# All eleven column groups of the second SwiGLUs by seven products, the first prepared during the mixer's output projection

## The chip, the cores and the metric

The kernel runs on one core of one Trainium2 chip. The metric is the device time of one execution in microseconds, as the median of several runs. A profiled execution comes with a trace of every instruction: TensorE (PE in the rows: matmuls, and PEld, their weight loads), VectorE (DVE), ScalarE (ACT), GpSimd (POOL) and the DMA queue that SyncE (SP) issues.

## The reference

Two layers work on 512 tokens of width 1024, in float32. What matters here is what stands around the second SwiGLU of each layer:

```python
h = h + merged @ w_o[i]                                                   # end of the mixer
h = h + 0.5 * swiglu(rmsnorm(h, ffn2_norm[i]), ffn2_w_gu[i], ffn2_w_down[i])
gate = jax.nn.sigmoid(rmsnorm(h, ple_norm[i]) @ w_ple_gate[i])

def swiglu(x, w_gu, w_down):
    g, u = jnp.split(x @ w_gu, 2, axis=-1)                                # 1024 -> 2 x 2816
    return (jax.nn.silu(g) * u) @ w_down                                  # 2816 -> 1024
```

## The kernel before

The activations lie transposed: `h[0]` to `h[7]` are 128 features by 512 tokens each, and a weight tile of 128x128 is the stationary operand. Each float32 product is made of three matmuls on rounded halves: a value is split into a rounded high part and the rest, and hi*hi, hi*lo and lo*hi are added up in PSUM (`mm3`, L266). The high part is a copy on ScalarE (L71, L260, L263), the low part a subtraction on VectorE (L72, L261, L264). Weights come as tiles of 128x1024 (512 KB, `Stream.raw`) into ten buffers (tag `st`, which the weight sums `s` use too), and the split ones lie in four pairs of buffers (`wh`, `wl`, `N_WH = 4`). So a new weight split on ScalarE waits until TensorE has read the split of four tiles before.

A SwiGLU has 22 blocks of 128 gate columns and as many up columns. Two neighbouring blocks, gate and up, make a **quad**: `Sevens` computes it by Strassen's way with seven products instead of eight, on halves of the inner dimension, of the tokens (256 and 256) and of the columns. `Quad` loads four quarters of the weights and forms four sums of them on VectorE (`part`: L149, L152, L154, L157). `Halved.row` makes the sums of the tokens: row j takes `h[j]` and `h[j+4]`, `own` the part that needs `h[j]` alone and `other` the rest; eight such operations on ScalarE and twelve on VectorE end in the split operands. `Sevens.step(n, j)` makes product j of quad n. Products 1, 2, 6, 3 and 4 are `joint`: 8 matmuls of 512 columns (L527: the weights' high part against the high and the low part of 256 tokens side by side) and 8 of 256 columns (L533: the low part). Products 5 and 7 are `product`, 24 matmuls of 256 columns each (L547).

The products of a quad share sums. `step` gathers product 1 in a PSUM pair `b`, copies it on ScalarE into the pair `a` (`seed`, L552) and adds product 2 there; product 6 goes on in `b`, which is then copied into the pair `d` for products 5 and 3; 7 and 4 end in `b`. `a` and `d` are the same two PSUM banks (pool `ap`, one buffer), so the seed of the one waits until the other has been read out (`out`, L556 on ScalarE and L557 on VectorE). After that `finish` scales by the norm's factor `r`, applies silu, multiplies (L603, L604, L608) and splits the result for the down projection. `down(m, f0, f1)` preloads a PSUM bank with 2*`h[m]` (L640), adds blocks f0 to f1 and writes `h[m]` back halved (L644); `fill` makes one such piece between two products of a quad. `next_quad` orders the steady part: quad n's product 4 stands behind quad n+1's product 1, and fills stand behind 4, 6 and 3.

Except in the very first SwiGLU, two of the 22 blocks (0 and 1) are not done by a quad but whole: `projs` and `proj` make 4 x 8 x 3 = 96 matmuls of 512 columns. Block 0 stands at the start of the SwiGLU, block 1 in two halves between the products of the first quad: whole gate and up of block 0, norm, 1 of quad 1, gate of block 1, 2 and 6, up of block 1, 5, 7, 3. The rest are ten quads.

Before that the mixer's output projection makes eight products of 24 matmuls (L1058 to L1060), `m0wop` in layer 0: each adds its result to `h[m]` on VectorE (L1060). As each `h[m]` is done, `normed` splits it (L263, L264), squares it (L333, L336), adds up the squares (L337), and, from `h[4]` on, makes two of the four token rows (`early=2`). `rms` turns the sum of squares into the factor `r` by two matmuls and a chain of ScalarE and VectorE operations (L350 to L354), with a load of an activation table ahead of it.

The order of each engine's instructions is set when the program is built, by a scheduler that may move an instruction ahead of others that it expects to wait; on the chip each engine takes its instructions in that order.

Of the kernel before, what the change touches and what calls it, by code (L numbers as in the profile page):

```python
# [129 lines left out]
class Quad:  # L130


    def __init__(self, W, quarters):
        self.W = W
        for q in ("a11", "a21", "a22", "a12"):
            setattr(self, q, W.raw(quarters[q]))

    def part(self, j):

        W = self.W  # L140
        tt = W.nc.vector.tensor_tensor
        if j == 1:
            return W.split(self.a11)
        if j == 2:
            return W.split(self.a12)
        if j == 4:
            return W.split(self.a22)
        if j == 3:
            tt(self.a12, self.a12, self.s, ALU.subtract)  # L149
            return W.split(self.a12)  # L150
        if j == 6:
            tt(self.a11, self.a11, self.a21, ALU.subtract)  # L152
# [6 lines left out]
        return W.split(self.a11)  # L159


# [21 lines left out]
def trunk_kernel(ctx, tc, dims, x, p, positions, gains, rope_c, final_row, weights, out):  # L183
# [19 lines left out]
    class Banks:  # L203


        def __init__(self):
            self.scope, self.n = None, 0
# [148 lines left out]

    def normed(nm, l, name, after=None, paired=True):

        xs, sq = [], Squares(name)
        for k in range(KD):  # L360
            xs.append(split(h[k], f"{name}x{k}", gain(nm, l, k), paired))
            sq.add(h[k])
            if after:
                after(k, xs)
        return xs, sq.parts()
# [130 lines left out]
    class Sevens:  # L496
# [62 lines left out]

        def step(self, n, j):  # L560
            d, H = self.quad(n), self.H
            if j == 1:
                d["b"] = PB(f"{self.name}{n}b")
                self.joint(d["b"], d, j)
                self.seed(n, "a")
            elif j == 2:
# [20 lines left out]

    def ffn(l, nm, name, first=False, beside=iter(()), early=2):

# [4 lines left out]
        ys = Halved(nm, l, name)  # L594
        n_whole = 4 if first else 2
        n0 = n_whole // 2
# [25 lines left out]

        xs, acc = normed(nm, l, name, early_rows)

# [26 lines left out]
        def fill():  # L651
            if downs:
                m, f0 = downs.pop(0)
                down(m, f0, f0 + 4)
# [12 lines left out]

# [9 lines left out]
        if first:  # L677
# [22 lines left out]
            activate(3)  # L700
            downs.extend((m, 0) for m in range(KD))
            fill()
# [5 lines left out]
            for _ in range(2):  # L708
                fill()
        else:  # L710
            pss[0] = whole(0)
# [18 lines left out]
        f0 = f_last  # L730
        left = [m for m in range(KD) if (m, f0) in downs]
        assert len(left) == len(downs)
# [25 lines left out]
    def mixer(l):  # L758
# [298 lines left out]
        banks.paired()  # L1057
        for m in range(KD):  # L1058
            ps = proj(W.col("w_o", l, m * P, D), merged, f"{name}wop{m}")
            nc.vector.tensor_tensor(h[m], ps, h[m], ALU.add)  # L1060
# [249 lines left out]
```

## Time and profile before

| what | us |
|---|---|
| median of 3 runs (2252.12 to 2252.79) | 2252.23 |
| profiled execution, its own time | 2252.33 |
| its span, first to last instruction | 2250.3 |
| busy: PE / DVE / ACT | 2240.8 / 1743.5 / 1456.1 |
| matmuls | 12144 |
| output projection of layer 0's mixer | 685.6 to 729.1 |
| start of the second SwiGLU of layer 0, to the end of its first quad's product 3 | 729.1 to 768.5 |

The page says 100% for PE, but a busy PE is not PE at its peak: a matmul of 512 columns is shown with 389 ns, and the next one starts some 227 ns later. So the starts of neighbouring matmuls are what to read. A row of the timeline has its start in us from the start of the span, its length, engine, line and operation; behind it in brackets the idle time before it and what ended it. Neighbours on ACT and DVE overlap by about 0.1 us, so that their spacing is the length less that.

### The profile page before, as it was taken

What the parts mean: (1) busy time and instruction counts of PE and PEld (TensorE: products, weight loads), DVE (VectorE), ACT (ScalarE), POOL (GpSimd) and SP (SyncE); (2) the same over time, 40 slices, a digit from 0 to 9 for tenths busy, and PEclk for the clock granted to TensorE, in tenths of its full rate; (3) what the DMA queues carried; (4) which work ended last, traced back from release to release, by engine and by line L of the source; (5) the groups of instructions that cost most, each with busy time, mean ns of one, the idle gap of its engine ahead of it and who ended that gap; (6) DMA issues with size and microseconds to landing.
All of it is one profiled execution on the core that took longest, in us unless ns stands there. A gap on an engine that the chain in (4) does not pass through costs nothing.

```text
span 2250.3 us, 31142 instructions
## 1 busy us (share of the span) xinstructions
PE 2240.8 (100%) x12144; PEld 1947.7 (87%) x12144; DVE 1743.5 (77%) x2453; ACT 1456.1 (65%) x2246; POOL 37.4 (2%) x42
## 2 busy tenths in 40 slices
PE   9999999999999999999999999999999999999998
PEld 8888888888888888888888888888888888888887
DVE  8987768788866887776798777687889678777756
ACT  7666666576744666667676666764767357666664
POOL 0000000000200000000000000000001000000000
PEclk9999999999999999999999999999999999999999
DMA  5333332323132232334223233323222223333321
GB/s 215 99 113 104 103 122 75 112 76 104 47 104 84 94 103 97 107 107 141 75 94 104 96 106 108 113 88 102 92 76 75 94 75 103 104 104 103 108 99 38
DMA packets 63362, 223.04 MB, mean 99 GB/s; under 512 B 7280, under 2 KB 7280, under 8 KB 63216
## 3 DMA queue, kind: packets, MB, share of 16 engines
q1 hardware_dynamic: 62640, 220.28, 29.2%
q8 instruction: 95, 1.56, 0.3%
q10 hardware_dynamic: 576, 0.79, 0.1%
q14 instruction: 51, 0.42, 0.1%
HBM read 218.94 MB, written 2.10 MB: 98 GB/s over the span
## 4 chain that ended last, share of the span: by engine, by line
PE 97%; DVE 2%; ACT 1%; issue 0%; DVEq 0%
PE a0pd L268 2%; PE a1pd L268 2%; PE b0pd L268 2%; PE b1pd L268 2%; PE a0pd L269 2%; PE a0pd L270 2%; PE b1pd L269 2%; PE b0pd L269 2%; PE a1pd L269 2%; PE b1pd L270 2%; PE b0pd L270 2%; PE a1pd L270 2%; PE m0mop L268 1%; PE m1mop L269 1%; PE m0mop L269 1%; PE m1mop L270 1%
## 5 line engine op out<-in xcount | busy, mean ns | idle before, releaser
L72 DVE TENSOR_TENSOR wl<-st,wh 128x1024 fp32r<-128x1024 f32 (+1 forms) x508 | 614.7, 1212 | 227.5 <-ACT wh L71 224.1
L71 ACT CAST wh<-st 128x1024 fp32r<-128x1024 f32 (+1 forms) x507 | 527.9, 1044 | 306.6 <-PE m1Bp L269 13.9
L71 ACT CAST wh<-s 128x1024 fp32r<-128x1024 f32 x49 | 51.6, 1052 | 28.8 <-PE m1Cp L269 4.2
L72 DVE TENSOR_TENSOR wl<-s,wh 128x1024 fp32r<-128x1024 f32 x49 | 59.6, 1216 | 0.3 <-ACT wh L71 0.3
L152 DVE TENSOR_TENSOR st<-st,st 128x1024 f32<-128x1024 f32 x49 | 59.7, 1219 | 0.2
L154 DVE TENSOR_TENSOR s<-st,st 128x1024 f32<-128x1024 f32 x49 | 59.6, 1217 | 0.1
L149 DVE TENSOR_TENSOR st<-st,s 128x1024 f32<-128x1024 f32 x49 | 59.6, 1216 | 0.0
L157 DVE TENSOR_TENSOR st<-st,st 128x1024 f32<-128x1024 f32 x49 | 59.6, 1216 | 0.0
L644 ACT ACTIVATE h<-a0pd 128x512 f32<-128x512 f32 x40 | 23.7, 594 | 5.6 <-PE a0pd L270 5.3
L644 ACT ACTIVATE h<-b1pd 128x512 f32<-128x512 f32 x40 | 23.7, 592 | 4.9 <-PE b1pd L270 4.8
L644 ACT ACTIVATE h<-b0pd 128x512 f32<-128x512 f32 x40 | 23.7, 592 | 4.7 <-PE b0pd L270 4.6
L644 ACT ACTIVATE h<-a1pd 128x512 f32<-128x512 f32 x40 | 23.6, 591 | 4.5 <-PE a1pd L270 4.4
L640 ACT ACTIVATE a1pd<-h 128x512 f32<-128x512 f32 x40 | 24.0, 599 | 0.7
L640 ACT ACTIVATE b1pd<-h 128x512 f32<-128x512 f32 x40 | 23.9, 599 | 0.6
L640 ACT ACTIVATE b0pd<-h 128x512 f32<-128x512 f32 x40 | 23.9, 598 | 0.6
L640 ACT ACTIVATE a0pd<-h 128x512 f32<-128x512 f32 x40 | 23.9, 598 | 0.6
L107 POOL MEMSET wh<- 128x256 f32 x4 | 1.1, 314 | 1173.3 <-DVE wl L72 1173.3
L268 PE MATMUL a0p<-a0x,wh 128*128 128x512 f32 x44 | 17.1, 390 | 0.0
L269 PE MATMUL a0p<-a0x,wh 128*128 128x512 f32 x44 | 17.1, 390 | 0.0
L270 PE MATMUL a0p<-a0x,wl 128*128 128x512 f32 x44 | 17.1, 389 | 0.0
L263 ACT ACTIVATE b0x<-h,cols 128x512 fp32r<-128x512 f32 x8 | 5.8, 724 | 13.3 <-DVE h L1060 13.3
L263 ACT ACTIVATE b1x<-h,cols 128x512 fp32r<-128x512 f32 x8 | 5.8, 723 | 13.3 <-DVE h L1060 13.3
(6945 smaller groups left out, 7503.9 us busy)
## 6 DMA issues: line engine op xcount, KB each, us to landing
st<-in_weights SPq DMA_DIRECT2D x406, 512.0 KB, 3.3
h<-in_x SPq DMA_DIRECT2D x8, 256.0 KB, 5.4
st<-in_weights SPq DMA_DIRECT2D x7, 256.0 KB, 5.3
out<-e1d SPq DMA_DIRECT2D x4, 256.0 KB, 2.1
out<-fh SPq DMA_DIRECT2D x3, 256.0 KB, 2.2
e0pi<-in_p SPq DMA_DIRECT2D x2, 256.0 KB, 3.5
e1pi<-in_p SPq DMA_DIRECT2D x2, 256.0 KB, 3.8
fg<-in_final_row SPq DMA_DIRECT2D x2, 256.0 KB, 4.5
```

Of the source, the lines that this page charges most:

```text
L71: self.nc.scalar.copy(hi[:, w], src[:, w])
L72: self.nc.vector.tensor_tensor(lo[:, w], src[:, w], hi[:, w].bitcast(F32), ALU.subtract)
L149: tt(self.a12, self.a12, self.s, ALU.subtract)
L152: tt(self.a11, self.a11, self.a21, ALU.subtract)
L154: tt(self.s, self.a22, self.a11, ALU.subtract)
L157: tt(self.a21, self.a21, self.a22, ALU.add)
L263: nc.scalar.activation(hi, src, AF.Copy, scale=scale)
L268: nc.tensor.matmul(ps, wh, vh, start=first, stop=False, skip_group_check=seeded)
L269: nc.tensor.matmul(ps, wh, vl, start=False, stop=False, skip_group_check=seeded)
L270: return nc.tensor.matmul(ps, wl, vh, start=False, stop=last, skip_group_check=seeded)
L640: nc.scalar.mul(ps, h[m], 2.0)
L644: nc.scalar.mul(h[m], ps, 0.5)
```

## The change

The second SwiGLUs of both layers (`ffn2`, the ones behind the mixers) do all 22 blocks by eleven quads (`quads=True`); no block is done whole. The first quad's weights are loaded and prepared ahead of the norm: `Quad.early` makes the three splits that need no sums first (a11, a12, and after two sums s), and all four sums. These three splits go to buffers of their own, in two pieces of 512 columns each (`pieces`, `Pieces`), which are split with 512-column operations. The three others are split through the four pairs as before.

The output projection makes its products in the order 0, 4, 1, 5, 2, 6, 3, 7 (`halfway`), so that row j of the token sums can start at once behind each second product, and three rows instead of two are made early (`early=3`). Its first two products go into the two halves of one PSUM pair (`first_two`).

Behind it comes: the `own` part of row 3, product 1 of quad 0, the norm, the `other` part of row 3, product 2 of quad 0, product 1 of quad 1 (its seed is left for later: `seeded=False`), products 6, 5, 7, 3 of quad 0. The down projection's first piece is cut in two: blocks 0 and 1 after quad 0, blocks 2 and 3 after quad 1 (`downs`), and `fill` makes two of the short pieces at a time.

```diff
 class Quad:
+    def early(self, split):
+        tt = self.W.nc.vector.tensor_tensor
+        self.ready[1] = split(self.a11)
+        self.ready[2] = split(self.a12)
+        tt(self.a11, self.a11, self.a21, ALU.subtract)
+        self.s = self.W.buffer("s")
+        tt(self.s, self.a22, self.a11, ALU.subtract)
+        self.ready[6] = split(self.s)
+        tt(self.a12, self.a12, self.s, ALU.subtract)
+        tt(self.a21, self.a21, self.a22, ALU.add)
+        self.summed = True
     def part(self, j):
+        if j in self.ready:
+            return self.ready.pop(j)
+        if self.summed:
+            return W.split({3: self.a12, 4: self.a22, 5: self.a21, 7: self.a11}[j])
...
-        n_whole = 4 if first else 2
+        n_whole = 4 if first else 0 if quads else 2
...
-        xs, acc = normed(nm, l, name, early_rows)
+        if quads:
+            def pieces(src):
+                parts = [split(src[:, c:c + 512], f"{name}q{c}") for c in (0, 512)]
+                return Pieces([a for a, _ in parts]), Pieces([b for _, b in parts])
+
+            sevens.quad(0)["w"].early(pieces)
+        xs, acc = normed(nm, l, name, early_rows, order=halfway if quads else range(KD))
...
-                step(n if j == 4 else n + 1, j)
-                if j == 6 and n % 2:
-                    downs.extend((m, 2 * n - 2) for m in range(KD))
+                if n == 0 and j == 1 and quads:
+                    sevens.seed(1, "a")
+                else:
+                    step(n if j == 4 else n + 1, j)
+                if j == 6 and (n % 2 or quads and n == 0):
+                    downs.extend((m, max(2 * n - 2, 2 if quads and n else 0), 2 * n + 2) for m in range(KD))
...
+        elif quads:
+            for j in range(early, KD // 2):
+                ys.own(j, xs)
+            step(0, 1)
+            r = rms(acc, D, name)
+            for j in range(early, KD // 2):
+                ys.other(j, xs)
+            step(0, 2)
+            step(1, 1, False)
+            for j in (6, 5, 7, 3):
+                step(0, j)
...
         banks.paired()
-        for m in range(KD):
-            ps = proj(W.col("w_o", l, m * P, D), merged, f"{name}wop{m}")
+        first_two = halves(PA(f"{name}wop"))
+        for i, m in enumerate(halfway):
+            ps = proj(W.col("w_o", l, m * P, D), merged, f"{name}wop{m}", first_two[i] if i < 2 else None)
             nc.vector.tensor_tensor(h[m], ps, h[m], ALU.add)
...
-        ffn(l, "ffn2", f"b{l}")
+        ffn(l, "ffn2", f"b{l}", early=3, quads=True)
```

At three places the built order of the instructions is of use (lines of the change are 31 to 58 higher than before at the same code: L1060 has become L1118, L260 L291, L552 L583, L556 L587).

First, VectorE around the end of the output projection's first product. Before:

```order
L261 TENSOR_TENSOR m0mg7l<-m0g_5048,m0mg7h 128x512
L72 TENSOR_TENSOR wl_6676<-st_6673,wh_6675 128x1024
L1060 TENSOR_TENSOR h_89<-m0wop_6564,h_89 128x512
L264 SCALAR_TENSOR_TENSOR b0x_6820<-h_89,cols,b0x_6820 128x512
L72 TENSOR_TENSOR wl_6708<-st_6705,wh_6707 128x1024
```

and now, VectorE again (`b0q0`, `b0q512` are the pieces of the first quad's splits, `h_89` is `h[0]`):

```order
L292 TENSOR_TENSOR m0mg7l<-m0g_5048,m0mg7h 128x512
L292 TENSOR_TENSOR b0q0l<-st_6819,b0q0h 128x512
L292 TENSOR_TENSOR b0q512l<-st_6819,b0q512h 128x512
L292 TENSOR_TENSOR b0q0l<-st_6825,b0q0h 128x512
L145 TENSOR_TENSOR st_6819<-st_6819,st_6821 128x1024
L72 TENSOR_TENSOR wl_6675<-st_6672,wh_6674 128x1024
L1118 TENSOR_TENSOR h_89<-m0wop,h_89 128x512
```

Between the last operation of the mixer's merge and the addition to `h[0]` there stood one operation; now five stand there. On TensorE the second product's first matmul waits for that addition, since both products lie in one PSUM pair, and seven matmuls of the third product (`m0wop_6627`) have been put ahead of it:

```order
L301 MATMUL m0wop<-m0mg7h,wl_6580 128x512
L299 MATMUL m0wop_6627<-m0mg0h,wh_6610 128x512
L300 MATMUL m0wop_6627<-m0mg0l,wh_6610 128x512
L301 MATMUL m0wop_6627<-m0mg0h,wl_6611 128x512
L299 MATMUL m0wop_6627<-m0mg1h,wh_6610 128x512
L300 MATMUL m0wop_6627<-m0mg1l,wh_6610 128x512
L301 MATMUL m0wop_6627<-m0mg1h,wl_6611 128x512
L299 MATMUL m0wop_6627<-m0mg2h,wh_6610 128x512
L299 MATMUL m0wop<-m0mg0h,wh_6579 128x512
```

Before, each product had a PSUM bank of its own, and the second followed the first at once.

Second, ScalarE from the norm on. Before (`b0u_6_7017` is the split of row 3 that product 6 needs):

```order
L469 ACTIVATE b0x_7003<-h_92,cols 128x512
L350 ACT_TABLE_LOAD
L350 ACTIVATE b0r<-b0ps,eps_t 128x512
L483 ACTIVATE b0y_7009<-h_96,cols 128x512
L351 ACTIVATE b0t<-b0r 128x512
L352 ACTIVATE b0ms<-b0ps,eps_t 128x512
L260 CAST b0t3h<-b0t_7004 128x512
L552 COPY b01a<-b01b 128x1024
L260 CAST b0u_6_7017<-b0u_7010 128x256
```

and now (`b0u_6_7011` is the same split, `b00a` and `b00d` are quad 0's pairs `a` and `d`, `b0pd_0` and `b0pd_1` the preloads of the first two pieces of the down projection):

```order
L500 ACTIVATE b0x_6967<-h_92,cols 128x512
L680 ACTIVATE b0pd_0_7264<-h_89 128x512
L381 ACT_TABLE_LOAD
L381 ACTIVATE b0r<-b0ps,eps_t 128x512
L514 ACTIVATE b0y_7003<-h_96,cols 128x512
L382 ACTIVATE b0t<-b0r 128x512
L383 ACTIVATE b0ms<-b0ps,eps_t 128x512
L291 CAST b0t3h<-b0t_6968 128x512
L71 CAST wh_7182<-st_6823 128x1024
L291 CAST b0u_6_7011<-b0u_7004 128x256
L291 CAST b0u_4_7014<-b0u_7004 128x256
L587 COPY b00o_7033<-b00a 128x512
```

A preload of 512 columns has come in front of the table load, and a weight split stands where a seed stood. On TensorE there stood, between the norm's two matmuls and product 6, products 1 and 2 of quad 1 and half of block 1 (24 matmuls of 512 columns); now there stand the rest of product 2 of quad 0 and most of product 1 of quad 1.

Third, ScalarE at a seed of the pair `a`. Before (quad 2, the first that has a quad ahead of it):

```order
L71 CAST wh_7374<-s 128x1024
L556 COPY b01o_7273<-b01d 128x512
L71 CAST wh_7400<-st_7398 128x1024
L552 COPY b02a<-b02b 128x1024
L604 ACTIVATE b01o_7273<-b01o_7273 128x256
```

and now (quad 1; `wh_7268` takes the buffer of the split of quad 0's product 3, `wh_7289` that of product 4):

```order
L71 CAST wh_7242<-s 128x1024
L71 CAST wh_7268<-st_7266 128x1024
L638 ACTIVATE b00c_7115<-b00c_7115 128x256
L587 COPY b00o_7170<-b00d 128x512
L71 CAST wh_7289<-st_7042 128x1024
L583 COPY b01a<-b01b 128x1024
L638 ACTIVATE b00o_7170<-b00o_7170 128x256
```

One weight split more stands ahead of the seed. On TensorE there stood product 1, product 4 and a piece of the down projection between product 3 of the quad ahead and the product 2 that adds to this seed; now there stands product 4 alone.

More of the change, by code (lines that the diff above doesn't have):

```diff
@@ L136, in __init__ @@
             setattr(self, q, W.raw(quarters[q]))
+        self.ready, self.summed = {}, False
+    def early(self, split):
[9 more added lines that the diff above has]
+        self.summed = True
     def part(self, j):
@@ L159, in part, with __init__, __getitem__ @@
         return W.split(self.a11)
+class Pieces:
+    def __init__(self, tiles):
+        self.tiles = tiles
+    def __getitem__(self, key):
+        rows, c = key
+        i, start = divmod(c.start, 512)
+        return self.tiles[i][rows, start:start + c.stop - c.start]
 class HiLo(tuple):
@@ L355, in rms, with normed @@
         return r
[L357 to L361, printed above, removed]
+    def normed(nm, l, name, after=None, paired=True, order=range(8)):
+        xs, sq = [None] * KD, Squares(name)
+        for k in order:
+            xs[k] = split(h[k], f"{name}x{k}", gain(nm, l, k), paired)
             sq.add(h[k])
@@ L558, in out, with step @@
             self.done(n, f, c, t, t)
-        def step(self, n, j):
+        def step(self, n, j, seeded=True):
             d, H = self.quad(n), self.H
@@ L564, in step @@
                 self.joint(d["b"], d, j)
-                self.seed(n, "a")
+                if seeded:
+                    self.seed(n, "a")
             elif j == 2:
@@ L586, in step, with ffn @@
                 self.out(n, d.pop("b"), 1, 0)
-    def ffn(l, nm, name, first=False, beside=iter(()), early=2):
+    halfway = (0, 4, 1, 5, 2, 6, 3, 7)
+    def ffn(l, nm, name, first=False, beside=iter(()), early=2, quads=False):
         H = S // 2
@@ L652, in fill @@
             if downs:
-                m, f0 = downs.pop(0)
-                down(m, f0, f0 + 4)
+                m, f0, f1 = downs.pop(0)
+                down(m, f0, f1)
+                if f1 == 2 and downs:
+                    m, f0, f1 = downs.pop(0)
+                    down(m, f0, f1)
         def next_quad(n):
@@ L700, in ffn @@
             activate(3)
-            downs.extend((m, 0) for m in range(KD))
+            downs.extend((m, 0, 4) for m in range(KD))
             fill()
@@ L730, in ffn @@
         f0 = f_last
-        left = [m for m in range(KD) if (m, f0) in downs]
+        left = [m for m in range(KD) if (m, f0, f0 + 4) in downs]
         assert len(left) == len(downs)
```

## Prediction

> **What bounds the kernel now.** I read the page first, then who waited for whom on TensorE, then busy time by stage, then the chain of waits around the first quad.
>
> ```profile
> span 2250.3 us, 31142 instructions
> PE 2240.8 (100%) x12144; PEld 1947.7 (87%) x12144; DVE 1743.5 (77%) x2453; ACT 1456.1 (65%) x2246; POOL 37.4 (2%) x42
> PE 97%; DVE 2%; ACT 1%; issue 0%; DVEq 0%
> ```
>
> ```profile
> PE idle L376 <- DVE hpi L305: 1.0, 1, 1.0
> PE m0cop L270 <- DVE wl L72: 0.3, 1, 0.3
> PE m1cop L270 <- DVE wl L72: 0.3, 1, 0.3
> ```
>
> TensorE sets the time: the chain is 97% its own, and in all its waits it loses 1.6 us. So a matmul less is gained in full, and any wait put in front of TensorE is lost in full, as there is no slack. By stage (output projection, then the start of the second SwiGLU; columns PE, PEld, DVE, ACT, POOL):
>
> ```profile
> 685.60:729.10 43.50, 43.50 (x193) 36.02 (x192) 30.26 (x45) 22.42 (x33) 0.00 (x0) 1.00 0.24 85
> 729.10:768.50 39.40, 39.40 (x212) 34.19 (x212) 33.70 (x48) 27.83 (x40) 0.00 (x0) 1.00 0.20 68
> ```
>
> TensorE is never idle in either, but VectorE has little room: 13.2 us in the first stage, 5.7 in the second.
>
> **TensorE's work.** The spacings, from the tile of the projection and the chain (start, length):
>
> ```profile
> L268 PE MATMUL m0wop<-m0mg0h,wh x8: 389/389/389, 685.6 to 723.7; 128*128 128x512 f32 x8
> ```
>
> ```profile
> 759.92 2.87 PE b01d L547 x24
> 762.80 2.88 PE b01b L547 x24
> 765.68 0.96 PE b01d L533 x8
> 766.64 1.84 PE b01d L527 x8
> ```
>
> From 685.6 to 723.7 are 7 x 24 matmuls: 0.227 us each. A joint product costs 0.96 + 1.84 = 2.80 us, a product of 24 narrow ones 2.87. Per layer the change takes away blocks 0 and 1, 96 x 0.227 = 21.8 us, and adds a quad, 5 x 2.80 + 2 x 2.87 = 19.7. Saved: 2.05 us a layer, **4.1 us in all**. The down projection keeps its matmuls, the weight loads their number; both are moved only.
>
> **Prices on the other engines.** Lengths with the overlap taken off (spacing) come from these rows, VectorE then ScalarE:
>
> ```profile
> 688.00 0.69 DVE L261 TENSOR_TENSOR m0mg7l<-m0g,m0mg7h 128x512 fp32r<-128x512 f32 x1 [0.76 <-ACT m0mg7h L260]
> 691.27 0.69 DVE L1060 TENSOR_TENSOR h<-m0wop,h 128x512 f32<-128x512 f32 x1 [0.59 <-PE m0wop L270]
> 729.35 0.69 DVE L1060 TENSOR_TENSOR h<-m0wop,h 128x512 f32<-128x512 f32 x1
> 729.96 1.22 DVE L152 TENSOR_TENSOR st<-st,st 128x1024 f32<-128x1024 f32 x1
> 731.09 0.75 DVE L264 SCALAR_TENSOR_TENSOR b0x<-h,cols,b0x 128x512 fp32r<-128x512 f32 x1
> 731.75 0.69 DVE L337 TENSOR_TENSOR b0acc<-b0acc,b0sq 128x512 f32<-128x512 f32 x1
> 732.35 1.22 DVE L72 TENSOR_TENSOR wl<-st,wh 128x1024 fp32r<-128x1024 f32 x1
> 733.49 0.69 DVE L261 TENSOR_TENSOR b0al<-b0acc,b0ah 128x512 fp32r<-128x512 f32 x1
> 744.28 0.43 DVE L485 TENSOR_TENSOR b0u<-b0t,b0x 128x256 f32<-128x256 f32 x1
> 744.74 0.42 DVE L486 TENSOR_TENSOR b0u<-b0y,b0u 128x256 f32<-128x256 f32 x1
> ```
>
> ```profile
> 732.47 0.62 ACT L260 CAST b0ah<-b0acc 128x512 fp32r<-128x512 f32 x1 [1.11 <-DVE b0acc L337]
> 740.46 0.72 ACT L469 ACTIVATE b0x<-h,cols 128x512 f32<-128x512 f32 x1
> 741.20 1.28 ACT L350 ACT_TABLE_LOAD   x1
> 742.49 0.69 ACT L350 ACTIVATE b0r<-b0ps,eps_t 128x512 f32<-128x512 f32 x1
> 743.08 0.71 ACT L483 ACTIVATE b0y<-h,cols 128x512 f32<-128x512 f32 x1
> 743.69 0.62 ACT L351 ACTIVATE b0t<-b0r 128x512 f32<-128x512 f32 x1
> 744.21 0.68 ACT L352 ACTIVATE b0ms<-b0ps,eps_t 128x512 f32<-128x512 f32 x1
> 744.78 0.62 ACT L260 CAST b0t3h<-b0t 128x512 fp32r<-128x512 f32 x1
> 745.29 1.02 ACT L552 COPY b01a<-b01b 128x1024 f32<-128x1024 f32 x1
> 753.11 0.58 ACT L556 COPY b01o<-b01a 128x512 f32<-128x512 f32 x1
> 759.74 1.05 ACT L71 CAST wh<-st 128x1024 fp32r<-128x1024 f32 x1 [2.85 <-PE b0pu L269]
> 783.51 0.61 ACT L644 ACTIVATE h<-b0pd 128x512 f32<-128x512 f32 x1
> 784.15 0.60 ACT L640 ACTIVATE b0pd<-h 128x512 f32<-128x512 f32 x1
> ```
>
> So on VectorE 0.60 for 512 columns, 0.67 with a scale, 1.13 for 1024, and 0.46 for 256 where each needs the one before; on ScalarE 0.53 for a split of 512, 0.95 for one of 1024. A result reaches another engine 0.04 us after its row's end; a matmul's result comes 0.16 after TensorE has gone on (389 less 227 ns), so 0.2 until ScalarE starts. The change adds to VectorE three weight splits and four sums per layer, 7 x 1.13 = 7.9 us, and pulls the first quad's preparation into the projection. The loads keep their number too:
>
> ```profile
> st<-in_weights SPq DMA_DIRECT2D x406, 512.0 KB, 3.3
> ```
>
> The first quad now holds five of the ten buffers through the projection (four tiles and s). Quad 1's four tiles take those of the projection's tiles, which come free one by one with their splits, the last some 20 us ahead of quad 1's product 2; a load of 3.3 us is hidden, and I count nothing. Without that cover each load would cost its 3.3 us.
>
> I walk through the built order of layer 0 on the clock of before, which holds up to the projection's start at 685.63. Layer 1 is the same.
>
> **Wait 1, second product of the projection.** VectorE starts the last merge operation at 688.00. Behind it come three splits of 512 (from 688.60), a sum (690.40), a weight split (691.53), and the addition to `h[0]` from 692.66 to 693.35; before, it ran at 691.27. TensorE ends the first product's issue at 691.07 and has 7 x 0.227 = 1.59 us of other matmuls, to 692.66. It resumes at 693.4: **0.75 us**. Bounds: 0 if the sum were elsewhere, 1.0 with a late weight cast. The additions that follow have TensorE's next products as cover; the projection ends at 729.9.
>
> **Wait 2, seed of quad 0.** Product 1 ends at 732.7. The copy takes 0.2 + 1.02, against five matmuls of quad 1, 1.14: **0.15** (0 to 0.3).
>
> **Wait 3, row 3 before product 6.** At 729.9 VectorE is still in a weight split, to 730.3. Then: the addition to `h[7]`, a square sum, a weight split, the scaled low part, the last square sum, 0.60 + 0.60 + 1.13 + 0.67 + 0.69: done at 734.0. ScalarE from 734.07: split of the sum 0.53, x of row 3 0.74, the preload 0.54, the table load 1.29, r 0.59, y 0.61, t 0.52, ms 0.57, t3 0.51, a weight split 0.95, at last the row's split for product 6, 0.4 long. That is ready at 741.3. TensorE does the norm at 735.8 (two matmuls of product 2 after it: 0.46), then 0.96, the 11 left of quad 1's product 1 (0.69 + 0.96), six of product 6 (0.72): it arrives at 739.6. Lost: **1.8** (1.4 to 2.2). Before, 24 matmuls of block 1 and two joint products, 11 us, stood there.
>
> ACT_TABLE_LOAD is followed by r after 1.29 us in these rows, with no gap. The Trainium skill ("ScalarE: Activation LUTs", What ACT_TABLE_LOAD costs) speaks against the change: it adds a drain of about 1380 ns to each switch; as an estimate from that page wait 3 would be 3.2 us. The row has no such drain.
>
> **Wait 4, seed for product 5.** Product 6 ends at 741.34 + 0.24 + 1.84 = 743.4, and product 5 follows at once. The copy must wait until VectorE has read `a`. Row 3's three sums stand on VectorE behind y (738.4) and end at 739.8; then VectorE has three 512 operations (1.80), two 256 splits (0.7), a weight split (1.13), then that addition (0.69): 744.1. The copy ends at 745.1: **1.7** (1.25 if VectorE is earlier than TensorE, 0.2 + 1.02 + 0.04; up to 2.0). Before, block 1's up half covered it.
>
> **Wait 5, seed of quad 1.** TensorE goes on from 745.1 with 5, 7, 3, 4: 2.87 + 2.88 + 2.80 + 2.80, to 756.5. ScalarE's weight split before the seed needs the buffer that product 4 reads last: 0.2 + 0.95 + 1.02 + 0.04 after TensorE has finished. **2.2** (2.0 to 2.5). Nothing stands between.
>
> **Wait 6, short pieces of the down projection.** Two banks alternate. Six matmuls, 1.36 us, now cover writing back and preloading, 0.52 + 0.60 + 0.3 in latencies, where 12 did before. **0.1 to 0.4** each time, some twice a layer behind other ScalarE work: I take 0.6 (0 to 0.9).
>
> Later quads have the old order. The sum per layer: 0.75 + 0.15 + 1.8 + 1.7 + 2.2 + 0.6 = 7.2 lost, 2.05 gained: +5.15. Both layers: +10.3. The profiled execution took 2252.33 (0.1 over the median): 2252.33 + 10.3 - 0.1 = **2262.5 us**. With all low bounds, 0 + 0 + 1.4 + 1.25 + 2.0 + 0 = 4.65, it is 2257.4; with all high ones, 8.9, it is 2265.9.
>
> **Rivals.** (A) Every wait finds cover. Then only the matmuls count: 2252.2 - 4.1 = 2248.1, a little faster. For it speaks that the kernel before loses nothing at the same places, and that ScalarE idles 21 us in the projection; against it that block 1, the cover of before, is what is removed. It decides where the waits stay below 2.05 us a layer.
> (B) VectorE and ScalarE get ahead, so that waits 1, 2, 3 and 6 vanish, and only the two seeds that the built order itself leaves uncovered remain: 1.25 + 2.2 = 3.45 a layer, less 2.05, twice: 2255.0, hardly to be told from before. Against it: the chain of wait 3 starts with the last `h`, and is twelve operations long.
> (C) The clock. After the end of the matmuls it is lower:
>
> ```profile
> 2240.00:2250.00 10.00, 2.37 (x20) 2.16 (x18) 5.34 (x19) 5.36 (x9) 0.00 (x0) 0.73 0.28 105
> ```
>
> With 5.7 us of waits between 739.6 and 758.7, the 13.4 us of matmuls there at 0.73 would take 5.0 us longer, both layers 9.9: 2272.4. The single waits are much shorter than the 7.6 us of idle in that last row. The Trainium skill ("TensorE: Matmul & The Clock Gate", HAM oscillation) puts the point at idle gaps over some 3.4 us; by that rule none of these waits would trip it, and no run here shows it.
> (D) The table load costs more than its row, at most as long again, 1.28 us, at wait 3: both layers 2.6, so 2265.1. Against it: r starts 1.29 us after the load does, with nothing between. By the figure of the Trainium skill's page named at wait 3 it would be 2265.3, as an estimate.
>
> **How the numbers follow.** Forecast 0.80, A 0.06, B 0.06, C 0.05, D 0.03. About 0.2% (4.5 us) can be told from no change. Slower by more than that are the forecast, C and D: 0.88; within it B and, as its 4.1 us lie at the bound, half of A: 0.09; faster the other half: 0.03. The range takes the forecast's bounds, and above a little for waits that I have not walked through: 2257 to 2267.5.
>
> **What would show it.** After: 12208 matmuls instead of 12144 (per layer 5 x 16 + 2 x 24 for 96); VectorE's addition to `h[0]` at about 692.7; TensorE waiting for ScalarE at `b0u` in product 6, at `b00d`, at `b01a`, each 1.5 to 2.5 us, in both layers; granted clock 1.00 throughout. It would be wrong if TensorE shows no waits in the 30 us behind the projection, or if a stage far from it has changed.

## The result, and the profile after

The changed kernel is slower. Six runs took 2264.57 to 2267.69 us, median 2266.36, beside 2252.63 (2252.12 to 2253.01) for the kernel before on the same chip: a ratio of 1.0061, 95% interval 1.0048 to 1.0074, or 13.7 us. Forecast were 2262.5 in a range of 2257 to 2267.5. The direction and nearly all waits came as worked out; 3.4 us are missing in the sum, and they have a cause that the forecast had taken for unlikely.

The page of the changed kernel, its span and busy times:

```profile
span 2264.8 us, 31380 instructions
...
PE 2243.9 (99%) x12208; PEld 1948.6 (86%) x12208; DVE 1765.3 (78%) x2485; ACT 1485.0 (66%) x2306; POOL 37.3 (2%) x42
```

The 12208 matmuls are those foretold. Where the 14.5 us of the profiled spans (2264.8 against 2250.3) lie is seen by the starts of each stage's first matmul in both traces (the last row runs to the start of the last matmul):

| stage, us | before | after |
|---|---|---|
| output projection, layer 0 / 1 | 43.52 / 43.52 | 44.47 / 44.47 |
| second SwiGLU, layer 0 / 1 | 339.17 / 339.17 | 345.62 / 345.57 |
| what follows it in layer 0 | 54.89 | 54.89 |
| first SwiGLU and mixer of layer 1 up to the projection | 676.82 | 676.84 |
| what follows the second SwiGLU in layer 1 | 59.37 | 59.39 |

So it is two stages and no others (the first projection starts at 685.63 before and at 685.43 after): 0.95 us a layer in the projection and 6.4 in the SwiGLU, although the latter has 2.2 us of matmuls less (96 x 0.227, less 40 x 0.227 and 88 x 0.120). Who waited for whom on TensorE (engine, line, in all, times, longest; layer 1 has the same rows with the same numbers; line numbers are now those of the changed kernel: L558 and L564 a joint product's wide and narrow matmuls, L578 products 5 and 7, L583 a seed, L1118 the addition to `h`):

```profile
PE b01a L558 <- ACT b01a L583: 2.0, 1, 2.0
...
PE b00b L564 <- ACT b0u L291: 1.5, 1, 1.5
...
PE b00d L578 <- ACT b00d L583: 1.5, 1, 1.5
...
PE m0wop L299 <- DVE h L1118: 0.6, 1, 0.6
```

These are waits 5, 3, 4 and 1. TensorE's timeline around three of them (start, length, what it is, idle before):

```profile
739.40 0.40 PE L564 MATMUL b00b<-b0u,b0q512l 128*128 128x256 f32 x2
741.32 0.50 PE L564 MATMUL b00b<-b0u,b0q512l 128*128 128x256 f32 x2 [1.52 <-ACT b0u L291]
...
745.14 0.39 PE L578 MATMUL b00d<-b0t0h,wh 128*128 128x256 f32 x1 [1.47 <-ACT b00d L583]
745.36 0.28 PE L578 MATMUL b00d<-b0t0l,wh 128*128 128x256 f32 x1
745.48 0.28 PE L578 MATMUL b00d<-b0t0h,wl 128*128 128x256 f32 x1
...
758.80 3.64 PE L558 MATMUL b01a<-b0x,wh 128*128 128x512 f32 x8 [2.05 <-ACT b01a L583]
762.24 1.19 PE L564 MATMUL b01a<-b0x,wl 128*128 128x256 f32 x8
```

Two things in these rows were not in the sum. After each wait the second matmul starts 0.1 us late (745.14 to 745.36 is 0.22, the next spacing 0.12). And the eight wide matmuls behind wait 5 take from 758.80 to 762.24: 0.43 us each instead of 0.227. That is half the clock, as the windows show (columns: from:to, length, busy time of PE, PEld, DVE, ACT, POOL, granted clock, DMA share, GB/s):

```profile
738.50:741.92 3.42, 1.90 (x15) 1.66 (x15) 3.35 (x8) 3.42 (x7) 0.00 (x0) 1.00 0.00 0
741.92:745.33 3.41, 1.94 (x9) 1.29 (x8) 2.78 (x5) 1.86 (x4) 0.00 (x0) 1.00 0.26 79
755.57:758.98 3.41, 1.36 (x7) 0.81 (x6) 3.38 (x5) 2.46 (x4) 0.00 (x0) 1.00 0.16 64
758.98:762.39 3.41, 3.41 (x9) 2.63 (x10) 2.53 (x5) 1.21 (x3) 0.00 (x0) 0.50 0.44 151
762.39:765.81 3.42, 3.42 (x24) 3.16 (x23) 1.56 (x2) 1.99 (x3) 0.00 (x0) 1.00 0.08 14
```

The clock is 0.50 for 3.41 us and then 1.00 again. In layer 1 it is 0.50 from 1881.97 to 1885.38. A stretch of 3.41 us at half the clock does the work of 1.7: 1.7 us a layer, **3.4 us in all**, which is what the sum lacks.

### The profile page after: what moved, and what is told of

It reads as the page before. It is cut to its first block, busy times and chain, and to the rows that moved or that the text cites. A ratio compares the mean times of both kernels' runs of the same rounds, so it can differ in the third digit from the quotient of the medians.

```text
span 2264.8 us, 31380 instructions
## 1 busy us (share of the span) xinstructions
PE 2243.9 (99%) x12208; PEld 1948.6 (86%) x12208; DVE 1765.3 (78%) x2485; ACT 1485.0 (66%) x2306; POOL 37.3 (2%) x42
## 4 chain that ended last, share of the span: by engine, by line
PE 95%; DVE 3%; ACT 1%; issue 1%; DMA 0%; SPq 0%; DVEq 0%; ACTq 0%
PE b0pd L299 2%; PE b1pd L299 2%; PE a0pd L299 2%; PE a1pd L299 2%; PE a0pd L300 2%; PE b1pd L300 2%; PE b0pd L300 2%; PE b1pd L301 2%; PE a0pd L301 2%; PE b0pd L301 2%; PE a1pd L300 2%; PE a1pd L301 2%; DVE wl L72 1%; PE m1mop L299 1%; PE m0mop L299 1%; PE m0mop L300 1%
## 5 line engine op out<-in xcount | busy, mean ns | idle before, releaser
L684 ACT ACTIVATE h<-b1pd 128x512 f32<-128x512 f32 x48 | 28.4, 594 | 4.1 <-PE b1pd L301 3.9
L684 ACT ACTIVATE h<-b0pd 128x512 f32<-128x512 f32 x48 | 28.4, 594 | 4.0 <-PE b0pd L301 3.8
L680 ACT ACTIVATE b1pd<-h 128x512 f32<-128x512 f32 x48 | 28.7, 601 | 0.7
L680 ACT ACTIVATE b0pd<-h 128x512 f32<-128x512 f32 x48 | 28.6, 600 | 0.7
L1179 PE MATMUL e1pg<-kh,e1x 128*128 128x512 f32 (+1 forms) x40 | 13.9, 349 | 0.0
```

The costliest lines, as they stand in the source:

```text
L680: nc.scalar.mul(ps, h[m], 2.0)
L684: nc.scalar.mul(h[m], ps, 0.5)
```

## The experiments

Nine kernels, each compared with the kernel before on its own chip, which took 2252.6 to 2252.8 there. Two of them measure the clock only.

### Wait 3 taken away: row 3 ahead of the norm

```diff
             step(0, 1)
-            r = rms(acc, D, name)
             for j in range(early, KD // 2):
                 ys.other(j, xs)
+            r = rms(acc, D, name)
             step(0, 2)
```

> Two statements change places: the second halves of row 3's token sums are written ahead of the norm, so that on ScalarE the scaling y of row 3 stands ahead of the table load, r and the rest, and row 3's splits for product 6 come earlier. Everything that is computed stays. Both theories: wait 3 goes (1.68 us a layer in the trace of the changed kernel, 3.4 in both layers), waits 1, 4 and 5 stay at 0.8, 1.6 and 2.2. Theory 'each wait for itself, and the lower clock comes from wait 5 alone': the granted clock behind wait 5 is again 0.5 to 0.7 for some 3.5 us, and the time is 2266.4 - 3.4 = 2263.0. Rival 'the lower clock needs the three waits within 20 us': without wait 3 the clock stays at 1.00 and the 1.7 us a layer that it costs go too: 2266.4 - 6.8 = 2259.6. Rival 'the lower clock has nothing to do with the waits': 2263.0 with the slow stretch at another place.

Measured: 2263.65 us (2260.63 to 2264.27, four runs), ratio to before 1.0045 (1.0028 to 1.0061). On ScalarE the scaling y of row 3 now stands ahead of the table load, and at product 6 TensorE is late by 0.2 instead of 1.7. ScalarE's timeline, then the windows around wait 5:

```profile
735.73 0.71 ACT L514 ACTIVATE b0y<-h,cols 128x512 f32<-128x512 f32 x1
736.46 1.28 ACT L381 ACT_TABLE_LOAD   x1
```

```profile
755.22:758.64 3.42, 1.43 (x6) 1.21 (x7) 2.68 (x4) 2.93 (x5) 0.00 (x0) 1.00 0.10 16
758.64:762.05 3.41, 3.41 (x15) 3.14 (x15) 2.43 (x4) 1.81 (x3) 0.00 (x0) 0.50 0.39 143
...
1874.80:1878.21 3.41, 1.36 (x7) 0.81 (x6) 3.21 (x6) 2.41 (x4) 0.00 (x0) 1.00 0.00 1
1878.21:1881.62 3.41, 3.41 (x13) 2.92 (x12) 1.99 (x3) 2.21 (x4) 0.00 (x0) 0.50 0.46 154
```

The second SwiGLU is 1.63 us shorter in layer 0 and 1.59 in layer 1; the lower clock stays. Wait 3 costs what its rows say, and the clock does not need three waits in 20 us.

### Waits 3 and 5 taken away: quad 1's first seed in two single banks

```diff
+class Apart:                      # w-th half of the pair in a bank of its own
...
+    def __getitem__(self, key):
+        rows, w, c = key
+        return self.tiles[w][rows, c]
...
+        def seed_apart(self, n, what):
+            d = self.todo[n]
+            d[what] = Apart([PS(f"{self.name}{n}{what}{w}") for w in range(2)])
+            for w in range(2):
+                nc.scalar.copy(d[what].tiles[w], d["b"][:, w, :])
...
             for j in (6, 5, 7, 3):
                 step(0, j)
+                if j == 7:
+                    sevens.seed_apart(1, "a")
...
-                if n == 0 and j == 1 and quads:
-                    sevens.seed(1, "a")
-                else:
+                if not (n == 0 and j == 1 and quads):
```

> Quad 1's first seed goes into two single banks that are free in this stretch, ahead of product 7 of quad 0, and not into the pair of banks that quad 0 holds until its product 3 has been read. This takes wait 5 (2.2 us a layer) away; as the short pieces' preloads no longer find these banks, ScalarE takes row 3's scaling ahead of the table load, and wait 3 (1.7) should go as well. New: the seed of quad 1's product 5 finds no piece of the down projection as cover: 0.2 + 1.02 + 0.04 = 1.3 at most. Theory 'the lower clock comes from the waits, wait 5 above all': clock 1.00 throughout, 2 x (1.7 + 2.2 + 1.7 - 1.3) = 8.6 less, 2257.8. Rival 'the clock is not from wait 5': a slow stretch of some 3.5 us remains and 2 x (1.7 + 2.2 - 1.3) = 5.2 goes: 2261.2. Rival 'the wait only moves to the next operation that the same chain on ScalarE feeds': TensorE waits about as long at quad 1's next product or at the first pieces, and the time stays above 2263.

Measured: 2258.43 us (2257.68 to 2258.81, ten runs), ratio 1.0025 (1.0015 to 1.0034). The waits of layer 0 in its profile that are over 0.6, but for the one at the program's start (layer 1 has the same two, of the same length):

```profile
PE b00d L589 <- ACT b00d L600: 1.3, 1, 1.3
PE b01d L589 <- ACT b01d L600: 1.1, 1, 1.1
```

Wait 4 is left (`b00d`), waits 3 and 5 are gone, and the new wait for quad 1's second seed (`b01d`) has come as expected. No stretch of these two stages is below a clock of 1.00. The time is that of the theory (2257.8) and not that of the same waits at half the clock (2261.2): together with the run above, in which wait 3 alone was gone and the lower clock stayed, this puts the 3.4 us down to wait 5. Its ten runs lie within 1.2 us, those of the changed kernel in two groups, 2264.6 to 2265.6 and 2267.1 to 2267.7. One stretch at half the clock more or less would part these groups; that is not shown, as only one of those runs has a trace.

### Wait 1 taken away: the early sums behind the first addition

```diff
-            sevens.quad(0)["w"].early(pieces)
+            with tc.issue_after(mixer.first):      # the addition to h[0]
+                sevens.quad(0)["w"].early(pieces)
...
-            nc.vector.tensor_tensor(h[m], ps, h[m], ALU.add)
+            added = nc.vector.tensor_tensor(h[m], ps, h[m], ALU.add)
+            if i == 0:
+                mixer.first = added.ins
```

> The first quad's early splits and sums may be issued on VectorE only behind the addition to h[0]; everything that is computed stays. Theory (the walk along VectorE's queue): wait 1 goes, 0.78 us a layer, 1.6 in both, the addition to h[0] comes back to about 691.3, waits 3 to 5 stay within 0.3 us: 2264.8. Rival 'VectorE is full in the projection': the 7.9 us of splits and sums only move on, and a later addition or wait 3 grows by as much: no change, 2266.4.

Measured: 2263.29 us (2262.71 to 2263.78, four runs), ratio 1.0046 (1.0031 to 1.0061): 3.1 less than the changed kernel, not 1.6. The addition to `h[0]` starts at 691.03, and the projection takes 43.69 in both layers, 0.78 less, as the theory has it. The rest is the clock again. Windows of layer 0, then of layer 1, each around wait 5:

```profile
755.11:758.53 3.42, 1.37 (x6) 0.85 (x5) 3.36 (x6) 2.30 (x3) 0.00 (x0) 1.00 0.08 32
758.53:761.94 3.41, 3.41 (x11) 2.78 (x10) 2.19 (x4) 1.67 (x3) 0.00 (x0) 0.50 0.50 159
...
1874.69:1878.10 3.41, 2.08 (x10) 1.40 (x9) 2.97 (x5) 2.46 (x5) 0.00 (x0) 1.00 0.36 139
1878.10:1881.52 3.42, 2.71 (x15) 2.37 (x16) 2.71 (x4) 2.67 (x5) 0.00 (x0) 1.00 0.39 132
```

The same wait of 2.2 us stands in both layers. In layer 1 it falls on the border of two stretches of 3.41 us, TensorE is busy 2.08 and 2.71 in them, and the clock stays. The SwiGLU takes 345.66 in layer 0 and 343.81 in layer 1.

### The early splits and sums taken away

```diff
-            sevens.quad(0)["w"].early(pieces)
+            sevens.quad(0)
```

> The first quad keeps no early splits and sums: each is done when its product needs it, as in all other quads; the order of the projection, three early rows and eleven quads stay. Theory 'the sums in the projection cost wait 1 and save more behind it': waits 1 and 2 go (0.9 a layer); VectorE has two sums and a split, 3 x 1.13 = 3.4 us, more to do ahead of product 6, while row 3 is being prepared, and a sum and splits more ahead of the products behind it. Up to 3.4 us are added to waits 3 and 4 together, I take 3.2: net + 2.3 a layer, + 4.6 in all, 2271.0. Rival 'wait 3 is ScalarE's chain alone': VectorE's extra work lies beside it, only wait 1 and 2 go, 2264.6.

Measured: 2271.12 us (2269.22 to 2272.29, four runs), ratio 1.0080 (1.0065 to 1.0095). The longest of TensorE's waits in layer 0 (in layer 1 it is as long):

```profile
PE b00b L564 <- ACT b0u L291: 3.3, 1, 3.3
```

Wait 3 is 3.3 instead of 1.5. The edit takes away the early weight splits as well as the sums, so the time alone does not say which of them matters. The timelines ahead of product 6 do. ScalarE takes up the row's split at 740.86 in the changed kernel and at 742.86 here:

```profile
740.86 0.71 ACT L291 CAST b0u<-b0u 128x256 fp32r<-128x256 f32 x2
```

```profile
735.13 1.04 ACT L71 CAST wh<-st 128x1024 fp32r<-128x1024 f32 x1
...
741.82 0.61 ACT L680 ACTIVATE b0pd<-h 128x512 f32<-128x512 f32 x1
...
742.86 0.95 ACT L291 CAST b0u<-b0u 128x256 fp32r<-128x256 f32 x2
```

```profile
742.01 0.42 DVE L516 TENSOR_TENSOR b0u<-b0t,b0x 128x256 f32<-128x256 f32 x1
```

ScalarE has no gap between 731.58 and the row's split. Its split of the sum of squares starts at 734.61 instead of 734.07, and behind it stand a weight split (735.13) and a preload (741.82) more: 0.54, 0.95 and 0.53, which make the 2.0 us. VectorE, with its sums, has the row's sum ready at 742.43, 0.4 before ScalarE comes to it. So wait 3 is still ScalarE's chain, and VectorE is the next limit, close behind.

The theory put the loss down to VectorE, and its time was met partly by luck: waits 3 and 4 together have grown by 2.4 us in layer 0 and 1.7 in layer 1, not by 3.2, and half the clock lasts longer. It follows wait 3 here, from 744.48 for 6.83 us and from 1867.46 for 3.41, and none follows wait 5. The early preparation costs wait 1, 1.6 us in both layers, and is worth more than that: by the medians it saves 4.8 net, the lower clock included.

### The two blocks kept

```diff
-        n_whole = 4 if first else 0 if quads else 2
+        n_whole = 4 if first else 2
...
-            sevens.quad(0)["w"].early(pieces)
+            sevens.quad(n0)["w"].early(pieces)
```

The order behind it and the pieces of the down projection are then those of before.

> The changed kernel's preparation (the first quad's early splits and sums, three rows of token sums in the projection, the halfway order), but the SwiGLU behind the mixer keeps its two plain blocks and ten quads, so that the matmuls are those of before. Theory 'the two blocks were the cover': waits 2 to 5 and the lower clock are gone, only wait 1 stays, 0.78 us a layer: 2252.6 + 1.6 = 2254.2. Rival 'the preparation itself delays ScalarE and VectorE': waits of 1.5 us or more stay at product 6 or at the seeds also with the blocks: 2257 or more.

Measured: 2254.63 us (2254.08 to 2255.07, ten runs), ratio 1.0009 (1.0000 to 1.0018). TensorE's waits over 0.3, but for the one at the program's start:

```profile
PE m1wop L299 <- DVE h L1118: 0.6, 1, 0.6
PE m0wop L299 <- DVE h L1118: 0.6, 1, 0.6
```

With the 96 matmuls in place all of waits 2 to 6 are gone, although ScalarE and VectorE do the same preparation. The blocks, with the order that belongs to them, were the cover.

### Single waits of chosen length, twice

Into the kernel before, 32 waits are built, one in each of eight quads of every SwiGLU:

```diff
                 self.product(d["b"][:, :, :H], d, j)                  # product 7
+                if (self.name, n) in self.held:
+                    z = G(f"{self.name}{n}z", F32R)[:, :P]
+                    nc.gpsimd.tensor_scalar(z, d["c5"].rearrange("p w t -> p (w t)")[:, :P], 0.0, None, ALU.mult)
+                    for _ in range(self.held[self.name, n]):
+                        nc.gpsimd.tensor_scalar(z, z.bitcast(F32), 0.0, None, ALU.mult)
+                    barrier[0] = mat(d["d"][:, 0, :H], z, self.ys[7][0][0], start=False, ...).ins
```

`mat` is the matmul instruction, issued behind the last barrier; `held` gives 4 to 11 repetitions in the first kernel and 2 to 5 in the second.

> The kernel before, with 32 single waits built in, one in each of eight quads of every SwiGLU, some 34 us from one to the next: behind product 7, TensorE does one more matmul of 256 columns whose weights are zeros, and these zeros come out of a chain of 5 to 12 short operations on GpSimd that starts when the quad's c5 is there; no later matmul may overtake it. What the kernel computes stays, but for these added zeros; its time is of no interest, only each wait's length and the matmuls' spacing behind it (0.227 us for 512 columns at full clock, 0.43 at half). The waits should come out between some 1 and 5 us. Theory 'a single wait of about 2 us lowers the clock, depending on where it falls': none of the waits under some 1.7 us is followed by a slow stretch, of those between 1.8 and 3 a part, of those over 3.5 all, and each slow stretch is about 3.4 us long and costs 1.7 whatever the length of the wait. Rival 'it takes several waits within 20 us': single waits of 2 to 3 us are followed by none. By the rule of the Trainium skill ('TensorE: Matmul & The Clock Gate', HAM oscillation) only waits over some 3.4 us are followed by one.

> The kernel before with 32 single waits as in the longer series, but shorter: chains of 3 to 6 GpSimd operations, so that the waits should be about 1.0, 1.6, 2.2 and 2.8 us, eight of each. The added zeros apart, what is computed stays. Theory 'the clock is set anew every 3.413 us, and falls for the next 3.413 us where more than about 2.0 us of such a stretch were idle': none of the sixteen waits below 1.7 is followed by a slow stretch; of those of 2.2 and 2.8 just those are of which over 2.0 us fall into one stretch of the grid that the clock record shows, by the share of positions some 4 in 10 and 6 in 10; and each slow stretch is 3.41 long. Rival 'the wait's own length decides': all of one length behave alike. Rival 'it needs several waits within 20 us': none of the 32.

GpSimd was slower than reckoned, so the waits are 2.0 to 9.1 us in the first kernel and 0.6 to 4.8 in the second. By the waits view, and whether a stretch at 0.50 follows:

| wait, us | first kernel: number, followed by half clock | second kernel |
|---|---|---|
| 0.6 to 1.0 | none | 8, 0 |
| 2.0 | 1, 1 | 7, 1 |
| 2.5 | none | 1, 1 |
| 3.2 | 3, **0** | 8, **8** |
| 4.4 and more | 28, 28 | 8, 8 |

Every stretch at half the clock that has full clock on both sides is 3.41, 6.83 or 10.24 us long, and in one run all of them begin on one grid of 3.413 us. The waits of 3.2 decide between the theories, since one length behaves in both ways. One of the first kernel, then two of the second (the latter in part), in windows on the grid of its own run (POOL, the fifth number, is the chain that is waited for):

```profile
1065.80:1069.21 3.41, 1.80 (x16) 1.59 (x14) 2.62 (x4) 1.42 (x2) 2.71 (x4) 1.00 0.35 115
1069.21:1072.62 3.41, 1.83 (x12) 1.74 (x13) 2.70 (x3) 0.42 (x1) 1.45 (x2) 1.00 0.10 38
1072.62:1076.03 3.41, 3.41 (x16) 2.81 (x16) 1.14 (x2) 1.53 (x2) 0.00 (x0) 1.00 0.00 0
```

```profile
932.56:935.98 3.42, 1.19 (x10) 0.98 (x9) 2.62 (x4) 1.46 (x2) 3.09 (x5) 1.00 0.47 156
935.98:939.39 3.41, 2.45 (x10) 2.42 (x11) 2.08 (x3) 0.00 (x0) 0.91 (x1) 0.50 0.00 0
939.39:942.80 3.41, 3.41 (x9) 2.64 (x8) 0.00 (x0) 0.12 (x1) 0.00 (x0) 0.50 0.00 0
942.80:946.22 3.42, 3.42 (x16) 2.78 (x15) 2.66 (x4) 2.28 (x3) 0.00 (x0) 1.00 0.02 5
...
2052.14:2055.55 3.41, 1.50 (x13) 1.29 (x11) 2.61 (x4) 1.41 (x3) 3.01 (x4) 1.00 0.40 145
2055.55:2058.96 3.41, 2.13 (x10) 2.13 (x11) 2.40 (x3) 0.12 (x1) 1.15 (x2) 0.50 0.02 8
```

In the first kernel the wait lies half in one stretch of the grid and half in the next, TensorE is busy 1.80 and 1.83 in them, and nothing follows. In the first row of the second 2.2 us of it lie in one stretch, 1.19 are left busy, and the next two stretches run at half. So neither the wait's length alone decides nor a heap of waits, but how busy TensorE was in a stretch that begins where it will. The border lies between 1.5 and 1.7 us of busy time in 3.41, as the view counts it: at 1.50 or less the clock fell each time, above 1.7 never, between them it did both. My shares of 4 and 6 in 10 for the lengths were of no use, as a length comes again after four quads, which take 41 steps of the grid almost exactly (138.20 to 278.06 is 40.97 steps), so that like waits fall on like places. The Trainium skill says that this window is 3.413 us long and free-running ("TensorE: Matmul & The Clock Gate", Part 1), which the traces bear out; its rule of thumb, which names only gaps over some 3.4 us (HAM oscillation, same page), is too lenient here: wait 5 is 2.2.

### All waits covered

The seed of quad 1 as above (now behind product 5 instead of 7), the early splits and sums behind the first addition as above, and another order of products:

```diff
-            for i, j in enumerate((1, 4, None, 2, 6, None, 5, 7, 3, None, None)):
+            for i, j in enumerate((1, None, 2, 6, 4, 5, 7, None, 3, None, None) if quads and n == 0 else
+                                  (1, 4, None, 2, 6, None, 5, 7, 3, None, None)):
```

> The changed kernel, eleven quads, with its waits covered one by one: the early splits and sums behind the addition to h[0]; quad 1's first seed in the two single banks, so that quad 1's product 2 can stand between products 6 and 5 of quad 0; product 4 of quad 0 behind product 6 of quad 1, as cover for that quad's second seed; the first pieces of the down projection one product later. Theory 'the loss is these waits and the clock that they lower, nothing else': waits of at most 0.2 to 0.5 us remain at five places, some 1.2 a layer, the clock stays at 1.00, and the 4.1 us of matmuls saved show: 2252.6 + 2.4 - 4.1 = 2250.9, a little faster than before. Rival 'what is taken off one wait comes back at the next, as ScalarE and VectorE have no time to spare there': 2256 or more.

Measured: 2252.24 us (2251.82 to 2252.68, eleven runs), ratio 0.9998 (0.9989 to 1.0007). No wait is over 0.3 in the two stages:

```profile
PE b00b L575 <- ACT b0u L302: 0.3, 1, 0.3
PE b10b L575 <- ACT b1u L302: 0.3, 1, 0.3
```

The whole loss of 13.7 us is gone, so nothing of it lies outside these waits and the clock behind them. But it is not the gain of 1.7 that was expected. The SwiGLU takes 338.87, 0.3 less than before, of 2.2 that the matmuls save: by the spacings 1.9 us a layer are still lost, at some seven places of 0.1 to 0.45 with 0.1 for the restart behind each. The waits were put too low, as the restarts were not counted.

One step further, quad 1's product 2 is also written between products 6 and 5, with its seed right behind its product 1:

```diff
-            for i, j in enumerate((1, None, 2, 6, 4, 5, 7, None, 3, None, None) if quads and n == 0 else
+            for i, j in enumerate((1, None, None, 6, 4, 5, 7, None, 3, None, None) if quads and n == 0 else
...
             step(1, 1, False)
-            for j in (6, 5, 7, 3):
+            sevens.seed_apart(1, "a")
+            step(0, 6)
+            step(1, 2)
+            for j in (5, 7, 3):
                 step(0, j)
-                if j == 5:
-                    sevens.seed_apart(1, "a")
```

> As the kernel with covered waits, but quad 1's first seed is written right behind its product 1, and its product 2 between products 6 and 5 of quad 0 in the program too, so that two of its matmuls stand inside product 6 as cover for row 3's splits. Everything that is computed stays. Theory 'what is left is only the small waits, each with 0.1 for the restart': of the 1.9 us a layer by which the covered kernel's second SwiGLU is over the sum of its matmuls, the wait for row 3 (0.45 + 0.1) goes and two or three of 0.2: 2252.2 - 2 x 0.9 = 2250.4, faster than before by about 2. Rival 'another small wait takes its place': 2252.2, no change.

Measured: 2251.07 us (2250.77 to 2251.79, eleven runs) beside 2252.81 (2252.11 to 2253.11), ratio 0.9993 (0.9984 to 1.0002). The runs of the two kernels do not overlap, but the interval holds 1, so that a gain of 1.7 us is likely and not shown. The SwiGLU takes 338.29, 0.9 less than before. It is the fastest kernel here, and the 4.1 us that the matmuls promise are at best half in hand.

## Why the prediction was right, and where it was short

| term, us a layer | foretold | measured |
|---|---|---|
| matmuls saved | 2.05 | 2.2 |
| wait 1, addition to `h[0]` | 0.75 | 0.78 + 0.1 restart |
| wait 2, seed of quad 0 | 0.15 | 0.1 + 0.1 |
| wait 3, row 3 | 1.8 | 1.7 + 0.1 |
| wait 4, seed for product 5 | 1.7 | 1.6 + 0.1 |
| wait 5, seed of quad 1 | 2.2 | 2.2 |
| wait 6, short pieces | 0.6 | 0.5 + 0.3 |
| half clock behind wait 5 | none | 1.7 |

Measured is the start-to-start time less the spacing at full clock. Together that is 2 x (9.3 - 2.2) = 14.2 beside 14.5 in the spans.

**The walk along the queues held.** The addition to `h[0]` was put at 692.7 and started at 692.49, behind the very operations that were named (VectorE's timeline; the projection began 0.2 us earlier than in the trace before, so that measured from there the two differ by 0.03):

```profile
690.22 1.23 DVE L145 TENSOR_TENSOR st<-st,st 128x1024 f32<-128x1024 f32 x1
691.35 1.23 DVE L72 TENSOR_TENSOR wl<-st,wh 128x1024 fp32r<-128x1024 f32 x1
692.49 0.69 DVE L1118 TENSOR_TENSOR h<-m0wop,h 128x512 f32<-128x512 f32 x1
```

Wait 3 was put at an end of 741.3, and product 6 went on at 741.32; wait 4 at 745.1, and product 5 began at 745.14. All six waits, restarts included, lie within the bounds given. What the prediction rested on most, that the two blocks were the cover, the run with the blocks kept shows, and the one with all waits covered shows that another order can stand in for them.

**The step that failed is the clock.** Rival C was given 0.05, with 0.73 over all 13.4 us of matmuls between the waits; against it stood that the single waits are much shorter than the 7.6 us of idle at the end of before, and the rule of the Trainium skill named there. Both arguments asked how long a wait is. What counts is how much of a fixed stretch of 3.41 us is idle: for wait 5 it left 1.36 us busy, and for waits 3 and 4 it left 1.90 and 1.94, which is why only the fifth was punished. So C happened in part, in another size: 0.50, for 3.41 us, and 3.4 in all instead of 9.9. The forecast and C were not alternatives, as the sum of chances had it, and the sign "granted clock 1.00 throughout" did not come.

The row that C rested on was misread. Its 0.73 is a mean over a stretch at 1.00 and one at 0.50, and the clock did not need the 7.6 us of idle in it. On the grid, the trace before shows the clock fall behind a stretch with 2.25 us of idle, about as long as wait 5:

```profile
2241.20:2244.62 3.42, 1.17 (x10) 0.96 (x8) 2.76 (x10) 3.16 (x6) 0.00 (x0) 1.00 0.41 153
2244.62:2250.27 5.65, 0.00 (x0) 0.00 (x0) 1.64 (x7) 1.02 (x2) 0.00 (x0) 0.50 0.25 93
```

**That the time lies in the range is luck.** With the waits and the matmuls as measured and no lower clock it would be 2263.1, near the forecast. The 2266.36 measured are more than the sum of all high bounds, 2265.9; what holds them in the range is the 1.6 us added for waits that were not walked through, and no such wait filled them, but the clock. The highest of the six runs, 2267.69, lies outside. How much the clock takes also hangs on where its stretches begin: in the run without wait 1 the same wait 5 cost it in one layer only.

**Small terms.** The restart of 0.1 after each wait was missing, some 0.7 us a layer in all; the saving was put 0.1 too low.

**The rivals.** A and B did not come: no wait found cover, and waits 1 and 3 did not vanish. D did not come: r starts 1.30 us after the table load, and the load stands in the middle of ScalarE's unbroken row (ScalarE's timeline).

```profile
735.82 1.28 ACT L381 ACT_TABLE_LOAD   x1
737.12 0.69 ACT L381 ACTIVATE b0r<-b0ps,eps_t 128x512 f32<-128x512 f32 x1
737.70 0.71 ACT L514 ACTIVATE b0y<-h,cols 128x512 f32<-128x512 f32 x1
```

The drain of 1380 ns of which the Trainium skill speaks ("ScalarE: Activation LUTs", What ACT_TABLE_LOAD costs) shows here as little as before.

## What to carry to other kernels

Work that looks replaceable may be the cover of chains on other engines: before 20 us of matmuls are taken out, list which copies and splits end under them, and what will stand there instead. Each new wait on a saturated TensorE costs its own length and 0.1 us, and 1.7 us or more on top where it leaves TensorE busy for less than about 1.6 us of a fixed stretch of 3.41. As nobody chooses where the stretches begin, a wait between about 1.8 us (3.41 less 1.6) and 3.6 (twice that) is to be priced with both outcomes.

## What the runs showed of the hardware that was not expected

The granted clock of TensorE knows 1.00 and 0.50 here, changes only on a grid of 3.413 us, and goes by the stretch that has just passed: from 1.00 it fell behind 1.50 us busy and less, and stayed behind 1.77 and more. It comes back only behind a stretch that is busy nearly throughout: in the rows of the second kernel with built-in waits 2.45 us busy, from 935.98, were not enough, so that the next stretch ran at 0.50 as well. A wait of 3.2 us cost nothing but itself three times and a slow stretch eight times. Several short waits in one stretch count together: in the first of those kernels a wait of 1.6 with smaller ones beside it left 1.68 busy and was followed by 0.50. After a wait the second matmul starts 0.1 us late. The windows of that wait of 1.6:

```profile
2110.28:2113.69 3.41, 1.68 (x11) 1.24 (x10) 2.52 (x5) 2.37 (x4) 0.00 (x0) 1.00 0.74 219
2113.69:2117.11 3.42, 3.42 (x19) 3.42 (x18) 0.32 (x1) 0.00 (x0) 0.00 (x0) 0.50 0.46 139
```
